# Seven block products in place of eight for the gate and up projections of a two-layer decoder trunk

## The chip, the cores and the metric

The kernel runs on one core of one Trainium2 chip. The metric is the time of one execution on the device in microseconds (us); several runs of the same kernel are taken and their median is quoted. A profile is one more execution, recorded instruction by instruction on each engine: TensorE (PE, with its weight loads as PEld), VectorE (DVE), ScalarE (ACT), GpSimd (POOL) and SyncE (SP), which here issues the loads from memory.

## What is computed

Two decoder layers over 512 tokens of width 1024. A layer has four sub-layers, each with an RMS norm in front and one behind: a feed-forward block, a token mixer (block-sparse attention beside retention), cross-attention into 256 memory tokens, and a second feed-forward block. The change is in the feed-forward blocks, of which there are four in all:

```python
D_MODEL = 1024; SEQ = 512; DEPTH = 2; D_FF = 2816

def swiglu(x, w_gate, w_up, w_down):
    return (jax.nn.silu(x @ w_gate) * (x @ w_up)) @ w_down

def rms_norm(x, g):
    xf = x.astype(jnp.float32)
    y = xf * lax.rsqrt(jnp.mean(xf * xf, axis=-1, keepdims=True) + EPS)
    return (y * g.astype(jnp.float32)).astype(x.dtype)

# in each layer, twice:
# x = x + 0.5 * rms_norm(swiglu(rms_norm(x, pre_g), w_gate, w_up, w_down), post_g)
```

All data are float32.

## The kernel before

Activations lie with features on the 128 partitions and the 512 tokens along the free axis: `x[c]`, eight tiles for 1024 features. Every large product is made of three matmuls in a reduced float32 type: each operand is split into a rounded part and the rest (`hi`, `lo`), and `mm3` adds hi·hi, hi·lo and lo·hi into one PSUM tile. The split of a weight tile of 128x1024 (`unit`: one load on SP's queue into `raw`, ACT writes `hi`, DVE writes `lo` = raw − hi) is done as the weights stream in; three `raw`, four `hi` and four `lo` buffers rotate. A normed input is not scaled before its product: `split_x` splits x times the gain of each feature, and the factor of each token (`bc`, from `prenorm`) is applied behind the product.

A feed-forward block (`ffn`) goes over the 22 blocks of 128 hidden features in three groups (8, 7, 7). For each block f the gate and the up product are 8 x 3 matmuls each, with 512 tokens moving past a stationary 128x128 weight tile. Then DVE and ACT form silu(gate)·up and split it into `hh`, `hl`. When a group is done, the down product adds its blocks into the eight output tiles y[c], again 512 tokens at a time; y is kept in SBUF and added to by DVE. In the last block of the kernel the first f and the last group are done in two halves of 256 tokens. Behind the last group: `sumsq`, `rms_cols`, and `postnorm`, which for each c forms yn (DVE), adds it to x (POOL, the first on DVE) and splits the new x for the next sub-layer. Products with the memory tokens (`mem_keys`, `mem_values`) are put in as fillers at the changes of sub-layer.

The program is written in order; a planner orders each engine's instructions before the run by its own costs, and places waits on semaphores where one engine needs another's result. On an engine the order is then fixed. SBUF is shared out in slots: tag `b` 24 tiles of 128x512, `xs` 16, `h` 16; PSUM as four tiles `acc` and four tiles `aux`.

The order of the two instructions that recur most:

```python
act.activation(hi, raw, AF.Copy)                                  # L85, whi
dve.tensor_tensor(lo, raw, hi.bitcast(F32), op=ALU.subtract)      # L86, wlo
```

Of the kernel before, what the change touches and what calls it, by code (L numbers as in the profile page):

```python
# [25 lines left out]
GROUPS = ((0, 8), (8, 15), (15, 22))  # L26
# [21 lines left out]
def trunk(ctx: ExitStack, tc: tile.TileContext, a: dict, out: bass.AP):  # L48
# [9 lines left out]
    slots = {"b": 24, "xs": 16, "h": 16, "kv": 6}  # L58
# [20 lines left out]
    def unit(src, n):  # L79

        raw = wp.tile([P, 1024], F32, name="raw", tag="raw", bufs=3)[:, :n]
        nc.sync.dma_start(raw, src)
        hi = wp.tile([P, 1024], F32R, name="whi", tag="whi", bufs=4)[:, :n]
# [5 lines left out]
    def raw_unit(src, n):  # L89
        raw = wp.tile([P, 1024], F32, name="raw", tag="raw", bufs=3)[:, :n]  # L90
        nc.sync.dma_start(raw, src)
        return raw
# [3 lines left out]
    nc.sync.dma_start(x[0], a["xT"][0])  # L96
    first = {0: unit(a["ffn1_gu"][0, 0, 0], 1024)}
    for c in range(1, 4):
        nc.sync.dma_start(x[c], a["xT"][c])
    first[1] = unit(a["ffn1_gu"][0, 0, 1], 1024)  # L100
    for c in range(4, NC):
        nc.sync.dma_start(x[c], a["xT"][c])
    nc.sync.dma_start(cst, a["consts"])
# [9 lines left out]
    def mm3(ps, ah, al, bh, bl, start, stop):  # L113
        pe.matmul(ps, ah, bh, start=start, stop=False)  # L114
        pe.matmul(ps, ah, bl, start=False, stop=False)  # L115
        pe.matmul(ps, al, bh, start=False, stop=stop)  # L116
# [40 lines left out]
    def rms_cols(ssq, n, width):  # L157
# [9 lines left out]
        return newton(v, nt)  # L167
# [17 lines left out]

    def gcols(l, col):
        return small[l][:, col : col + NC]

    def prenorm():

        xh, xl = [h for h, _ in xs], [lo for _, lo in xs]
        xs.clear()
        ssq, part = None, None
# [9 lines left out]
        return xh, xl, cols, bc  # L203

    def postnorm(y, ssq, gains, nxt, ts_=slice(0, T)):

        w = ts_.stop - ts_.start
        ps = row_bc(rms_cols(ssq[:, ts_], D, w), w // P)
        for c in range(NC):
# [3 lines left out]
            split_x(c, nxt, ts_)  # L213
# [43 lines left out]
    def ffn(l, which, gains, nxt, filler=None, prep=None, halves=False):  # L257
        gu, dn = FF_UNITS[which]
        if filler:
            filler()  # L260
        xh, xl, cols, bc = prenorm()
        y, ssq = [None] * NC, None
        for gi, (f0, f1) in enumerate(GROUPS):
            hh, hl = [], []
            for f in range(f0, f1):
                w = [first.pop(b) if b in first else unit(a[gu][l, f, b], 1024) for b in range(2)]
                pss = [acc("ps_gu") for _ in range(2)]
                for ts_ in HALVES if halves and f == 0 else (slice(0, T),):
                    for (wh, wl), ps in zip(w, pss):
                        for k in range(NC):  # L270
                            s = slice(k * P, (k + 1) * P)
                            mm3(ps[:, ts_], wh[:, s], wl[:, s], xh[k][:, ts_], xl[k][:, ts_], k == 0, k == NC - 1)
                g1 = big("g1")
                dve.tensor_tensor(g1, pss[0], bc, op=ALU.mult)  # L274
                th = big("th")
                act.activation(th, g1, AF.Tanh, scale=0.5)
                u1 = big("u1")
                dve.tensor_tensor(u1, pss[1], bc, op=ALU.mult)  # L278
                dve.scalar_tensor_tensor(g1, th, 1.0, g1, op0=ALU.add, op1=ALU.mult)
                dve.scalar_tensor_tensor(u1, g1, 0.5, u1, op0=ALU.mult, op1=ALU.mult)  # L280
                h_, l_ = split(u1, "h", tag="h")
                hh.append(h_)
                hl.append(l_)
            n = f1 - f0
            last = gi == len(GROUPS) - 1
            if prep and last:
                prep()
            if last and nxt is None:
                down_halves(a[dn][l], f0, n, hh, hl, y, gains)
                return  # L290
            for c in range(NC):
                wh, wl = unit(a[dn][l, c][:, f0 * P : f1 * P], n * P)
                ps = acc("ps_dn")
                for k in range(n):
                    s = slice(k * P, (k + 1) * P)
                    mm3(ps, wh[:, s], wl[:, s], hh[k], hl[k], k == 0, k == n - 1)
# [7 lines left out]
        postnorm(y, ssq, gains, nxt)  # L304

    def down_halves(src, f0, n, hh, hl, y, gains):

        w = []
        for c in range(NC):
            if c < 4:  # L310
                wh, wl = unit(src[c][:, f0 * P : (f0 + n) * P], n * P)
                w.append([(wh[:, k * P : (k + 1) * P], wl[:, k * P : (k + 1) * P]) for k in range(n)])
            else:
                raw = raw_unit(src[c][:, f0 * P : (f0 + n) * P], n * P)
                parts = []
                for k0 in (0, 4):
                    m = min(4, n - k0) * P
# [625 lines left out]
```

## Time and profile before

| what | value |
|---|---|
| median of three runs | 2507.27 us (2506.3 to 2509.06) |
| the profiled execution, its own time | 2508.29 us |
| its span, first to last instruction | 2506.5 us |
| mean granted clock of TensorE | 0.995 of full speed |
| PE, PEld, DVE, ACT, POOL busy | 97%, 81%, 56%, 36%, 10% of the span |

Times in the rows are in us from the start of the span, durations in us unless they are marked ns. "128x512 f32 x56 | 38.7, 691" means 56 instructions on tiles of 128 partitions by 512 elements, together 38.7 us, 691 ns each. Matmuls overlap, so the duration of one matmul is longer than the time from its start to that of the next; what a stretch of matmuls costs is the length of the stretch over their number.

### The profile page before, as it was taken

The numbers are of one execution on the slowest core, as the hardware profiler recorded it, in microseconds if no ns is written. First come the engines' busy times: TensorE is split into PE (matmuls) and PEld (weight loads), VectorE is DVE, ScalarE is ACT, GpSimd is POOL, SyncE is SP. The second block draws the span as 40 slices with busy tenths as digits, with TensorE's granted clock in tenths as the row PEclk, the third lists the DMA queues.
The fourth block names the chain that finished last, engine by engine and source line by source line (L and its number), as shares of the span: only waits on it lengthen the run. The fifth ranks groups of instructions, "written<-read, shape, count | busy, mean of one in ns | idle before, by whom it ended". The sixth has DMA issues, their size and how long they took to land. (4 is left out here: it accounts for less than half of the span.)

```text
span 2506.5 us, 30782 instructions
## 1 busy us (share of the span) xinstructions
PE 2431.5 (97%) x12052; PEld 2020.5 (81%) x12052; DVE 1400.2 (56%) x2536; ACT 902.4 (36%) x1480; POOL 258.8 (10%) x218
## 2 busy tenths in 40 slices
PE   8999999999999999999999999999999998999997
PEld 6888878888877878888878888868888777888887
DVE  6434458465776484344484344584657766634454
ACT  4322243255344443222343222332553443322222
POOL 0000022001040120000120000130010402100002
PEclk9999999999999999999999999999999999999999
DMA  4333333411232233233333333324112222232321
GB/s 173 98 100 94 99 121 108 143 45 34 76 109 84 93 101 93 101 93 100 110 98 96 101 93 101 106 89 150 44 35 70 93 76 68 86 100 92 102 90 62
DMA packets 74593, 233.62 MB, mean 93 GB/s; under 512 B 8272, under 2 KB 17744, under 8 KB 74448
## 3 DMA queue, kind: packets, MB, share of 16 engines
q1 hardware_dynamic: 65232, 222.21, 27.9%
q10 hardware_dynamic: 9216, 9.44, 1.2%
q8 instruction: 95, 1.56, 0.3%
q14 instruction: 50, 0.41, 0.1%
HBM read 229.53 MB, written 2.10 MB: 92 GB/s over the span
## 5 line engine op out<-in xcount | busy, mean ns | idle before, releaser
L85 ACT ACTIVATE whi<-raw 128x1024 fp32r<-128x1024 f32 (+2 forms) x402 | 417.8, 1041 | 1097.6 <-PE ps_gu L115 324.0
L86 DVE TENSOR_TENSOR wlo<-raw,whi 128x1024 fp32r<-128x1024 f32 (+2 forms) x402 | 491.2, 1223 | 292.7 <-ACT whi L85 284.4
L114 PE MATMUL ps_gu<-xsh,whi 128*128 128x512 f32 (+1 forms) x1424 | 552.3, 389 | 13.8 <-ACT whi L85 9.3
L115 PE MATMUL ps_gu<-xsl,whi 128*128 128x512 f32 (+1 forms) x1424 | 555.0, 390 | 9.9 <-DVE xsl L184 9.7
L116 PE MATMUL ps_gu<-xsh,wlo 128*128 128x512 f32 (+1 forms) x1424 | 552.8, 388 | 0.0
L115 PEld LDWEIGHTS ps_gu<-xsl,whi 128*128 128x128 f32 x1424 | 268.6, 189 | 71.2 <-DVE xsl L184 17.7
L114 PEld LDWEIGHTS ps_gu<-xsh,whi 128*128 128x128 f32 x1424 | 269.0, 189 | 69.2 <-ACT whi L85 9.2
L116 PEld LDWEIGHTS ps_gu<-xsh,wlo 128*128 128x128 f32 x1424 | 268.8, 189 | 55.4 <-DVE wlo L86 1.8
L154 POOL TENSOR_TENSOR ssq<-ssq,sq 128x512 f32<-128x512 f32 (+1 forms) x84 | 131.4, 1564 | 1708.7 <-ACT sq L153 1705.6
L115 PE MATMUL ps_dn<-hl,whi 128*128 128x512 f32 (+1 forms) x704 | 268.5, 382 | 2.4 <-DVE hl L123 2.4
L114 PE MATMUL ps_dn<-hh,whi 128*128 128x512 f32 (+1 forms) x704 | 268.2, 381 | 0.0
L116 PE MATMUL ps_dn<-hh,wlo 128*128 128x512 f32 (+1 forms) x704 | 268.0, 381 | 0.0
L278 DVE TENSOR_TENSOR u<-ps_gu,rstd_bc 128x512 f32<-128x512 f32 x88 | 60.8, 691 | 215.4 <-PE ps_gu L116 215.3
L274 DVE TENSOR_TENSOR g<-ps_gu,rstd_bc 128x512 f32<-128x512 f32 x88 | 60.8, 691 | 183.9 <-PE ps_gu L116 179.4
L115 PEld LDWEIGHTS ps_dn<-hl,whi 128*128 128x128 f32 x704 | 132.3, 188 | 28.9 <-DVE hl L123 3.8
L114 PEld LDWEIGHTS ps_dn<-hh,whi 128*128 128x128 f32 x704 | 132.4, 188 | 26.2 <-ACT hh L122 0.5
L116 PEld LDWEIGHTS ps_dn<-hh,wlo 128*128 128x128 f32 x704 | 132.4, 188 | 25.1
L301 DVE TENSOR_TENSOR y<-ps_dn,y 128x512 f32<-128x512 f32 x56 | 38.7, 691 | 132.3 <-PE ps_dn L116 132.3
L115 PE MATMUL ps_fm<-xsl,whi 128*128 128x512 f32 x256 | 103.2, 404 | 4.0 <-DVE xsl L184 3.8
L114 PE MATMUL ps_fm<-xsh,whi 128*128 128x512 f32 x256 | 103.0, 404 | 0.0
L116 PE MATMUL ps_fm<-xsh,wlo 128*128 128x512 f32 x256 | 101.3, 396 | 0.6 <-DVE wlo L86 0.6
L612 ACT ACTIVATE p<-p,smx 128x512 f32<-128x512 f32 (+3 forms) x128 | 70.5, 552 | 87.2 <-DVE smx L610 87.0
(226 smaller groups left out, 3723.0 us busy)
## 6 DMA issues: line engine op xcount, KB each, us to landing
raw<-in_ffn_gu_dram SPq DMA_DIRECT2D x176, 512.0 KB, 3.3
raw<-in_ffn_dn_dram SPq DMA_DIRECT2D x64, 448.0 KB, 3.3
raw<-in_ffn_dn_dram SPq DMA_DIRECT2D x32, 512.0 KB, 3.5
raw<-in_win_fm_dram SPq DMA_DIRECT2D x32, 512.0 KB, 3.3
raw<-in_wk_dram SPq DMA_DIRECT2D x16, 512.0 KB, 3.5
raw<-in_cmp_w_dram SPq DMA_DIRECT2D x16, 512.0 KB, 3.7
raw<-in_wout_dram SPq DMA_DIRECT2D x16, 512.0 KB, 3.5
raw<-in_wv_dram SPq DMA_DIRECT2D x16, 512.0 KB, 3.5
```

The lines of the kernel that those rows point to most:

```text
L85: act.activation(hi, raw, AF.Copy)
L86: dve.tensor_tensor(lo, raw, hi.bitcast(F32), op=ALU.subtract)
L114: pe.matmul(ps, ah, bh, start=start, stop=False)
L115: pe.matmul(ps, ah, bl, start=False, stop=False)
L116: pe.matmul(ps, al, bh, start=False, stop=stop)
L154: eng.tensor_tensor(acc_t, acc_t, sq, op=ALU.add)
L274: dve.tensor_tensor(g1, pss[0], bc, op=ALU.mult)
L278: dve.tensor_tensor(u1, pss[1], bc, op=ALU.mult)
L301: dve.tensor_tensor(y[c], ps, y[c], op=ALU.add)
L612: act.activation(pr[i], pr[i], AF.Exp, bias=m, scale=-1.0, accum_out=sums[:, i : i + 1])
```

## The change

The 2816 hidden features are taken in 11 pairs of blocks. For a pair, gate and up together are one product of a 2x2 block matrix of weights (two blocks of features by two halves of the 1024 inputs) with a 2x2 block matrix of inputs (two halves of the inputs by two halves of the 512 tokens). It takes eight block products by the usual rule and seven by Strassen's scheme (`p1` to `p7`). Each block product is 2 (gate, up) x 4 x 3 matmuls with 256 tokens moving. Sums of weight blocks are made by POOL in place in `raw`, before the split; sums of input blocks (`combos`) are made once for each feed-forward block; sums of products are made by DVE, ACT and POOL from PSUM. The up half is no longer scaled for each token; the factor is applied at the norm behind the block (`cols`). Gate and up of the first pairs are prepared ahead of the norm that precedes them (`ffn_first`). The down product follows after every two pairs (four blocks of h), so it has six groups, the last with one pair. Buffers: `b` 18, `xs` 24, `h` 8, `raw` 6.

```diff
-GROUPS = ((0, 8), (8, 15), (15, 22))
+NPAIR = NF // 2
+PAIRS = tuple(tuple(range(j, min(j + 2, NPAIR))) for j in range(0, NPAIR, 2))
-    slots = {"b": 24, "xs": 16, "h": 16, "kv": 6}
+    slots = {"b": 18, "xs": 24, "h": 8, "kv": 6, "onsa": 1}
...
+    def pair_tile(name):
+        t = wp.tile([P, 1024], F32, name=name, tag="raw", bufs=6)
+        return [t[:, :T], t[:, T:]]
...
-    def rms_cols(ssq, n, width):
+    def rms_cols(ssq, n, width, cols=None):
...
+        if cols is not None:
+            dve.tensor_tensor(t, t, cols[1], op=ALU.mult)
...
+    def direct(c, g, ts_=slice(0, T)):
+        k, top = c % 4, c < 4
+        if ts_.start == 0:
+            ops["x", c] = big("xg")
+        xg = ops["x", c]
+        act.activation(xg[:, ts_], x[c][:, ts_], AF.Copy, scale=g[:, c : c + 1])
+        if top:
+            if ts_.start == 0:
+                if k % 2 == 0:
+                    ops["t1", k // 2] = (big("x1h", F32R, tag="xs"), big("x1l", F32R, tag="xs"))
+                u = slice(k % 2 * 256, k % 2 * 256 + 256)
+                hi, lo = [t[:, u] for t in ops["t1", k // 2]]
+                act.activation(hi, xg[:, :256], AF.Copy)
+                dve.tensor_tensor(lo, xg[:, :256], hi.bitcast(F32), op=ALU.subtract)
+                ops[1, k] = hi, lo
+        else:
...
+            act.activation(hi, xg[:, ts_], AF.Copy)
+            dve.tensor_tensor(lo, xg[:, ts_], hi.bitcast(F32), op=ALU.subtract)
+            ops[3, k], ops[4, k] = [tuple(t[:, u] for t in ops["t3", k]) for u in HALVES]
+    def combos():
+        h7 = big("x7h", F32R, shape=(P, 4, T), tag="onsa")
+        for k in range(4):
...
+            pool.tensor_tensor(t7[:, :256], b[3], b[1], op=ALU.subtract)
+            dve.tensor_tensor(t5[:, :256], b[1], b[0], op=ALU.subtract)
+            dve.tensor_tensor(t5[:, 256:], b[3], t5[:, :256], op=ALU.subtract)
+            pool.tensor_tensor(t7[:, 256:], t5[:, 256:], b[2], op=ALU.subtract)
+            for o, t, hi in ((5, t5, None), (7, t7, h7[:, k])):
...
+                act.activation(hi, t, AF.Copy)
+                dve.tensor_tensor(lo, t, hi.bitcast(F32), op=ALU.subtract)
+                for u in range(2):
+                    ops[o + u, k] = hi[:, HALVES[u]], lo[:, HALVES[u]]
...
-        for c in range(NC):
+        for c in (0, 4, 1, 5, 2, 6, 3, 7) if nxt[0] else range(NC):
             t = big("yn")[:, :w]
             dve.scalar_tensor_tensor(t, y[c][:, ts_], gains[:, c : c + 1], ps, op0=ALU.mult, op1=ALU.mult)
             (dve if c == 0 else pool).tensor_tensor(x[c][:, ts_], x[c][:, ts_], t, op=ALU.add)
-            split_x(c, nxt, ts_)
+            follow(c, nxt, ts_)
...
+    class Pair:
...
+        def add(self, t, u):
+            pool.tensor_tensor(t, t, u, op=ALU.add)
+        def raw(self, n):
+            if n == 1:
+                self.a = self.load(0)
+            elif n == 2:
+                self.b = self.load(1)
+            elif n == 7:
+                self.c = self.load(2)
+                self.add(self.a, self.c)
+            elif n == 5:
+                self.d = self.load(3)
+                self.add(self.c, self.d)
+                return self.c
+            elif n == 6:
+                self.add(self.a, self.d)
+            elif n == 3:
+                self.add(self.a, self.b)
+            return self.b if n == 2 else self.d if n == 4 else self.a
...
+            for u in range(2):
+                for k in range(4):
+                    s = slice(u * 512 + k * P, u * 512 + (k + 1) * P)
+                    xh, xl = ops[o, k]
+                    mm3(ps[:, HALVES[u]], wh[:, s], wl[:, s], xh, xl, start and u == 0 and k == 0, u == 1 and k == 3, not start)
...
+        def p6(self):
+            self.product(6, self.B, 6, start=False)
+            self.e = big("ge")
+            dve.tensor_tensor(self.e, self.B, self.s1, op=ALU.subtract)
+            pool.tensor_tensor(self.s5, self.e, self.s5, op=ALU.subtract)
+        def p4(self):
+            self.product(4, self.C, 8, start=False)
+            dve.tensor_tensor(self.s7, self.e, self.s7, op=ALU.subtract)
+            dve.tensor_tensor(self.s5, self.s5, self.C, op=ALU.subtract)
+        def p3(self):
+            ps = acc("ps_gu")
+            self.product(3, ps, 4)
+            dve.tensor_tensor(self.e, ps, self.e, op=ALU.subtract)
+        def swiglu(self, bc, hs):
+            for q in ((self.A, self.e), (self.s5, self.s7)):
+                g1, th = big("g1"), big("th")
+                for ts_, t in zip(HALVES, q):
+                    dve.tensor_tensor(g1[:, ts_], t[:, :256], bc[:, ts_], op=ALU.mult)
+                act.activation(th, g1, AF.Tanh, scale=0.5)
+                dve.scalar_tensor_tensor(g1, th, 1.0, g1, op0=ALU.add, op1=ALU.mult)
+                for ts_, t in zip(HALVES, q):
+                    dve.tensor_tensor(g1[:, ts_], g1[:, ts_], t[:, 256:], op=ALU.mult)
+                hs.append(split(g1, "h", 0.5, tag="h"))
+    def ffn_first(l, which, filler=None):
+        def run():
+            if filler:
+                filler()
+            ps_ = warm[l, which] = [Pair(a[FF_UNITS[which][0]][l], j) for j in PAIRS[0]]
+            for n in (1, 2):
+                for p in ps_:
+                    p.weights(n)
+            ps_[0].r[7] = ps_[0].raw(7)
+        return run
...
+        for gi, js in enumerate(PAIRS):
+            if gi == 0:
+                ps_ = warm.pop((l, which))
+                for n in ("p1", "p2"):
+                    for p in ps_:
+                        getattr(p, n)()
+                for n in ("p7", "p5"):
+                    getattr(ps_[0], n)()
+                cols, bc = prenorm_rows()
...
+            for p in ps_:
+                for n in ("p1", "p7", "p5", "p2", "p6", "p4", "p3"):
+                    if gi > 0 or n not in ("p1", "p2") and (p is ps_[1] or n not in ("p7", "p5")):
+                        getattr(p, n)()
+                p.swiglu(bc, hs)
...
-        q = []
+        q = pair_tile("q") + pair_tile("q")
...
-            t = big("vr", tag="h")
+            t = big("vr", tag="xs")
```

## Rows read from the trace of the kernel before

**Rows 1.** The page, part 1: busy time of each engine, share, instructions.
```profile
PE 2431.5 (97%) x12052; PEld 2020.5 (81%) x12052; DVE 1400.2 (56%) x2536; ACT 902.4 (36%) x1480; POOL 258.8 (10%) x218
```

**Rows 2.** Busy time by stretch: length, PE, PEld, DVE, ACT, POOL, granted clock, DMA.
```profile
30.00:335.00 305.00, 305.00 (x1349) 252.52 (x1348) 142.22 (x172) 88.79 (x109) 0.00 (x0) 1.00 0.31 97
...
875.00:916.00 41.00, 36.88 (x204) 29.35 (x203) 36.37 (x61) 18.96 (x26) 16.85 (x10) 1.00 0.30 95
...
2110.00:2150.00 40.00, 31.71 (x188) 27.59 (x187) 33.00 (x83) 17.39 (x32) 15.69 (x17) 0.91 0.21 66
```

**Rows 3.** The same, PE, PEld, DVE on ps_gu (first) and ps_dn (others) alone.
```profile
145.00:221.20 76.20, 76.16 (x336) 62.88 (x336) 8.99 (x13) 1.00 0.30 92
...
221.30:259.30 38.00, 38.00 (x168) 31.22 (x167) 4.84 (x7) 0.00 (x0) 1.00 0.33 106
...
2476.60:2492.30 15.70, 15.70 (x131) 15.58 (x130) 2.44 (x6) 0.00 (x0) 1.00 0.20 68
```

**Rows 4.** Groups by line and shape: count | busy us, mean ns | idle before.
```profile
L86 DVE TENSOR_TENSOR wlo<-raw,whi 128x1024 fp32r<-128x1024 f32 x46 | 56.2, 1222 | 37.0 <-ACT whi L85 36.9
...
L301 DVE TENSOR_TENSOR y<-ps_dn,y 128x512 f32<-128x512 f32 x56 | 38.7, 691 | 132.3 <-PE ps_dn L116 132.3
...
L280 DVE SCALAR_TENSOR_TENSOR u<-g,u 128x512 f32<-128x512 f32 x88 | 61.2, 696 | 2.2
...
L123 DVE TENSOR_TENSOR hl<-u,hh 128x512 fp32r<-128x512 f32 x88 | 60.3, 685 | 9.8 <-ACT hh L122 9.8
...
L122 ACT ACTIVATE hh<-u 128x512 fp32r<-128x512 f32 x88 | 55.7, 633 | 63.2 <-DVE u L280 63.1
...
L329 DVE TENSOR_TENSOR y<-ps_dn,y 128x256 f32<-128x256 f32 x16 | 6.7, 422 | 18.9 <-PE ps_dn L116 18.7
...
L154 POOL TENSOR_TENSOR ssq<-ssq,sq 128x256 f32<-128x256 f32 x19 | 14.8, 777 | 654.4 <-ACT sq L153 654.1
```

**Rows 5.** Timeline of DVE within a group: start, duration, instruction, [idle before <- releaser].
```profile
2162.33 0.69 DVE L278 TENSOR_TENSOR u<-ps_gu,rstd_bc 128x512 f32<-128x512 f32 x1 [1.58 <-PE ps_gu L116]
2163.05 0.69 DVE L280 SCALAR_TENSOR_TENSOR u<-g,u 128x512 f32<-128x512 f32 x1
2163.66 1.22 DVE L86 TENSOR_TENSOR wlo<-raw,whi 128x1024 fp32r<-128x1024 f32 x1
2164.80 0.68 DVE L123 TENSOR_TENSOR hl<-u,hh 128x512 fp32r<-128x512 f32 x1
```

**Rows 6.** Timeline of POOL, and of DVE beside it, cross-attention to feed-forward.
```profile
354.74 1.29 POOL L154 TENSOR_TENSOR ssq<-ssq,sq 128x512 f32<-128x512 f32 x1 [2.18 <-ACT sq L153]
...
887.14 11.39 POOL L212 TENSOR_TENSOR x<-x,yn 128x512 f32<-128x512 f32 x7 [13.57 <-DVE yn L211]
898.49 5.66 POOL L154 TENSOR_TENSOR ssq<-ssq,sq 128x512 f32<-128x512 f32 x3
...
899.34 1.98 DVE L86 TENSOR_TENSOR wlo<-raw,whi 128x1024 fp32r<-128x1024 f32 x1
901.25 1.75 DVE L184 SCALAR_TENSOR_TENSOR xsl<-x,small,xsh 128x512 fp32r<-128x512 f32 x1
902.92 1.77 DVE L154 TENSOR_TENSOR ssq<-ssq,sq 128x512 f32<-128x512 f32 x1
904.62 0.74 DVE L184 SCALAR_TENSOR_TENSOR xsl<-x,small,xsh 128x512 fp32r<-128x512 f32 x1
905.28 0.68 DVE L154 TENSOR_TENSOR ssq<-ssq,sq 128x512 f32<-128x512 f32 x1
```

**Rows 7.** The same transition, ps_gu alone: length, PE, PEld, DVE, clock, DMA.
```profile
885.60:915.20 29.60, 22.15 (x85) 15.03 (x85) 0.00 (x0) 1.00 0.26 87
```

**Rows 8.** The end of the chain that ended last: start, duration, what.
```profile
2492.42 0.43 DVE y L329
...
2497.36 0.68 PE bc_ps L173 x2
...
2502.33 0.87 POOLq L938
```

More of the change, by code (lines that the diff above doesn't have):

```diff
@@ L111, in trunk, with mm3 @@
             lst.append(hg)
[L113 to L116, printed above, removed]
+    def mm3(ps, ah, al, bh, bl, start, stop, more=False):
+        pe.matmul(ps, ah, bh, start=start, stop=False, skip_group_check=more)
+        pe.matmul(ps, ah, bl, start=False, stop=False, skip_group_check=more)
+        pe.matmul(ps, al, bh, start=False, stop=stop, skip_group_check=more)
     def split(src, name, gain=None, tag="b"):
@@ L186, in gcols, with follow @@
+    def follow(c, nxt, ts_=slice(0, T)):
+        seven, g = nxt[:2]
+        (direct if seven else split_x)(c, g, ts_)
+        if seven and c == NC - 1 and ts_.stop == T:
+            combos()
     def gcols(l, col):
@@ L255, in out_halves, with __init__, load, weights @@
             postnorm(y, ssq, gains, nxt, ts_)
-    def ffn(l, which, gains, nxt, filler=None, prep=None, halves=False):
+    class Pair:
+        def __init__(self, src, j):
+            self.src, self.j, self.w, self.r = src, j, {}, {}
+        def load(self, q):
+            k = self.j, q
+            return first.pop(k) if k in first else raw_unit(self.src[self.j, q], 1024)
+        def add(self, t, u):
[17 more added lines that the diff above has]
+            return self.b if n == 2 else self.d if n == 4 else self.a
+        def weights(self, n):
+            self.w[n] = split_unit(self.r.pop(n) if n in self.r else self.raw(n))
+        def product(self, n, ps, o, start=True):
+            if n not in self.w:
+                self.weights(n)
+            wh, wl = self.w.pop(n)
+            for u in range(2):
[3 more added lines that the diff above has]
+                    mm3(ps[:, HALVES[u]], wh[:, s], wl[:, s], xh, xl, start and u == 0 and k == 0, u == 1 and k == 3, not start)
+        def kept(self, ps):
+            t = big("gk")
+            act.activation(t, ps, AF.Copy)
+            return t
+        def p1(self):
+            self.A = acc("ps_gu")
+            self.product(1, self.A, 1)
+            self.s1 = self.kept(self.A)
+        def p2(self):
+            self.product(2, self.A, 3, start=False)
+        def p7(self):
+            self.C = aux("ps_gc")
+            self.product(7, self.C, 7)
+            self.s7 = self.kept(self.C)
+        def p5(self):
+            self.B = acc("ps_gu")
+            self.product(5, self.B, 5)
+            self.s5 = self.kept(self.B)
+        def p6(self):
[21 more added lines that the diff above has]
+                hs.append(split(g1, "h", 0.5, tag="h"))
@@ L258, in ffn @@
+    warm = {}
+    def ffn_first(l, which, filler=None):
[8 more added lines that the diff above has]
+        return run
+    def ffn(l, which, gains, nxt, prep=None):
         gu, dn = FF_UNITS[which]
-        if filler:
-            filler()
-        xh, xl, cols, bc = prenorm()
@@ L262, in ffn @@
         y, ssq = [None] * NC, None
[L263 to L285, printed above, removed]
@@ new lines, in ffn @@
+        for gi, js in enumerate(PAIRS):
[7 more added lines that the diff above has]
+                cols, bc = prenorm_rows()
+                sq = tiny("cols2", NT)
+                dve.tensor_tensor(sq, cols, cols, op=ALU.mult)
+            else:
+                ps_ = [Pair(a[gu][l], j) for j in js]
+            hs = []
+            for p in ps_:
[3 more added lines that the diff above has]
+                p.swiglu(bc, hs)
+            f0, n = 2 * js[0], len(hs)
+            last = gi == len(PAIRS) - 1
@@ L818, in xattn @@
                     mm3(ps, v_h[:, fs], v_l[:, fs], pTh[m], pTl[m], m == 0, m == 1)
-                h_, l_ = split(ps, "xo", tag="h")
+                h_, l_ = split(ps, "xo", tag="xs" if f < 4 else "h")
                 oh.append(h_)
```

127 lines of the change are left out of this document (70 added, 57 removed).

## Prediction

> **What bounds the kernel now.** I read the page's busy shares first, then the stretches, then the groups, then the timeline where stretches meet. By the shares TensorE is busy for 97% of the span and no other engine for more than 56% [rows 1]. A matmul counts as busy longer than its place in the pipe, so I looked at a stretch: in 305 us inside a feed-forward block PE has no gap, DVE is busy 142 us, ACT 89 us and POOL not at all [rows 2]. So the inside of a block is bound by PE, and there the time follows the number of matmuls and the spacing of their starts. Where sub-layers meet it is another engine: in the 41 us from cross-attention to the second feed-forward block DVE is busy 36.4 us and POOL 16.9 us [rows 2], and 85 matmuls of gate and up took 29.6 us [rows 7] where inside a block they would take 19.3 us. A change that takes work from PE and gives it to DVE and POOL gains in the first kind of stretch and loses in the second.
>
> **The change part by part: matmuls.** 336 matmuls of 512 tokens take 76.20 us, 226.8 ns each; in the down product 168 take 38.00 us, 226.2 ns. 131 matmuls of 256 tokens, each with a weight load of its own, take 15.70 us, 119.8 ns [rows 3]. Halving the columns does not halve the cost: the two lines differ by 107 ns for 256 columns, and some 13 ns stay with every matmul. PEld is busy for 15.58 of those 15.70 us, so weight loads have no slack left, but they keep up. One pair before: 4 products x 8 x 3 = 96 matmuls x 226.8 = 21.77 us. After: 7 x 24 = 168 x 119.8 = 20.13 us. That is 7.5% less, not the eighth that the count of columns promises: 1.64 us. 43 pairs make 70.5 us. The 44th, first in the last block, has half of its 512-token matmuls split into halves today (48 x 226.8 + 96 x 119.8 = 22.39 us): 2.3 us. In that block the halved last group of down products shrinks from seven blocks to two: 360 x 226.2 + 336 x 119.8 ns = 121.7 us become 480 x 226.2 + 96 x 119.8 = 120.1 us: 1.6 us. Sum for PE: **74.4 us less**. Above 129.6 ns for a matmul of 256 tokens (96 x 226.8 / 168) nothing would be left of it.
>
> **Load on DVE and POOL in a pair.** Weight splits: 7 x 1.22 us where there were 4. Sums of products: three with an operand in PSUM (0.69 each) and one in SBUF (0.69). Gate: eight half-width steps of 0.42, two of 0.70, two splits of 0.69. Together 17.5 us of DVE; before it was 4 x 1.22 + 10 x 0.69 = 11.8 us [rows 4]. POOL: four sums of 128x1024, which the trace does not have; 256 columns take 0.78 us [rows 4] and 512 alone 1.29 [rows 6], so 1024 at the same slope 2.3 us, and one of 1.29: 10.5 us where there was nothing. The outputs y are added to by DVE five times in a block and not twice: 24 more at 0.69, 16.6 us a block. ACT gets some 3 splits and 3 copies more; it is at 36% and stays uncounted.
>
> POOL and DVE get in each other's way. Three additions on POOL, 1.29 us each alone, took 5.66 us; beside them a weight split took 1.98 (1.22 alone), an input split 1.75 (0.74), an addition 1.77 (0.68) [rows 4, 6]. Alone these would be 3.87 + 2.64 = 6.51 us; from 898.49 to 904.62 they took 6.13, a rate of 1.06, almost one after the other. I count POOL and the DVE instructions with two operands in SBUF as one queue. (The Trainium skill, SBUF — State Buffer, section "Who interferes with whom", has this as a lock: a DVE instruction with two SBUF inputs and a GpSimd instruction that reads SBUF exclude each other for a whole instruction. The trace agrees within those 6%; by the lock alone 6.13 would be 6.51, and the stretches below 6% longer.)
>
> A full group of two pairs: PE 2 x 20.13 + 96 x 0.226 = 62.0 us (65.3 before). The queue: DVE 2 x 14.5 + 4.9 for the down weights, POOL 21.0, together 54.9 us. It fits with 7 us to spare, so inside a block I keep PE as the bound.
>
> **Where a group turns to its down product.** The last product p3 has to become h before the third of four blocks can be multiplied: e 0.69, times bc 0.42, tanh 0.63 (as L122, the same shape), 0.70, two half steps 0.84, hi 0.63, lo 0.69: 4.6 us, with hand-overs of up to 0.1 as in [rows 5] 4.7 us. Now one step of the sort (u, product, split) hides behind seven earlier blocks. After it, PE has the first two blocks for three outputs, as many as PSUM has free: 18 x 0.226 = 4.1 us. It costs nothing if the planner finds more, 3.3 us if it keeps to one output at a time (6 matmuls, 1.4 us); I take 4.7 − 4.1 = 0.6, since the planner mixes accumulations already: 20 full groups, **12 us** (0 to 66). The last group of each block is one pair, and no h is ready: 4.7 us bare, four times, **18.8 us** (0 if memory products, put there as fillers, come early, to 24 with the other half of the pair's gate in the way).
>
> **The start of a block.** Count from the first yn, just before POOL's seven additions to x [rows 6]. Before, 29.6 us later 85 of the 192 matmuls of two pairs are done [rows 7]; the other 107 take 24.3 us, so the two pairs end at 53.9. After, four products (11.5 us) need only splits of x. The others need the sums of inputs, behind the last x at about 13 us: 8 half-width differences on each of DVE and POOL and 8 splits, to about 23 us. Then ten products, 28.8 us: 51.8 if nothing else is late, a cost of 1.2 us against the 3.3 gained in two pairs. But the queue has, up to there: POOL 7 x 1.29 + 8 x 0.78 + 3 x 1.29 + 7 x 2.3 + 2 x 1.29 = 37.8 us, DVE x 0.69, input splits 4 x 0.42 + 4 x 0.69, differences 3.4, their splits 5.5, squares 2.8, 15 weight splits 18.3, sums 1.4, gate of the first pair 5.3: 41.8 us. 79.6 us at the rate of 1.06 are 75 us. What is not due by then (gate 5.3, three down splits 3.7, a sum 1.3) or fits in the 13.57 us that POOL sat idle before [rows 6] (two weight splits 2.4) leaves 66.9, or 63 us: a cost of 12.4. Between 1.2 and 12.4 (24 if nothing can be put off) I take 6: the queue weighs here, but the first block has no additions to x, part of POOL's work lies under DVE instructions with an operand in PSUM (yn, e), and six of the sixteen late splits may slip behind products that wait anyway. Four blocks: **24 us** (5 to 56).
>
> **The rest.** At the end the last half has 48 matmuls (5.8 us) where it had 168 (20.1 us) over the norm of the first half. From the last matmul's sum (2492.42) to the last issue (2502.33) [rows 8] DVE carries everything; the first half's yn and additions now fall into it: **3 us** (0 to 8). Six more `xs` and fewer `b` slots: q and ksel move out of `b` by as many tiles in the mixer, so nothing there; in cross-attention nothing moves out, and a head could wait for one split (1.3 us, rows above, eight heads): 0, at most 10. Loads: the same bytes. A pause of PE can cost clock: with its bubble the start of the last block ran at a granted 0.91 [rows 2], which is 2.4 GHz with stretches of 1.2 GHz; 0, at most 4 us a block, within the bound of 56.
>
> Sum: −74.4 + 12 + 18.8 + 24 + 3 = −16.6 us on the profiled execution's 2508.29 us: 2491.7. That execution is 1.0 us above the median of the runs, so I give **2491 us**, 0.65% less.
>
> **Rivals.** *The queue of DVE and POOL sets the time* (slower). For it: rows 6, and the 36 of 41 us in which DVE is busy there already. Against: inside a block 7 us of each 62 are spare. A block's start costs 14 us, and as the products alone (40.3 us) face some 38 us of queue, each of the 16 later full groups slips by 1 us: −74.4 + 56 + 16 + 12 + 18.8 + 3 = +31, 2539 us (2512 to 2556). It decides from about 10 us a start. The skill's lock, above, would have this outcome if no work could be put off. *Everything is covered*: the planner fills the turns, and starts cost 1.2 us: −74.4 + 5 + 3 = −66, 2441 us. For it: no gap in 305 us today; against: a chain of 4.7 us with nothing ready in a one-pair group. *Gain and losses cancel*: a start costs 10 us: 2507. *It does not do what it says*, the matmuls coming no faster than 129.6 ns: 131 matmuls in a row speak against it; I give it no chance of its own.
>
> **How the numbers follow.** Forecast 0.40 (own range 2450 to 2501), all covered 0.12, cancelled 0.12, slower 0.36. What a measurement of this kernel can tell from no change is about 0.2%, 5 us. Faster 0.52, within 0.12, slower 0.36. The range leaves out the lower half or so of "all covered" and the upper quarter of the slow case: 2446 to 2546.
>
> **What would show it.** In the profile after: some 119.8 ns from start to start in ps_gu inside a block; PE still near 97%, or, if the queue wins, gaps before ps_gu released by DVE's whi/wlo or POOL's sums; POOL at 10 us a pair, weight splits near 1.22 us if they meet few of POOL's sums and near 2 us if many; a gap of 1 us at most before ps_dn in a full group and of 4 to 5 us in the last; two pairs done 55 to 60 us after the first yn. I am wrong if the starts cost over 10 us, or if the turns cost 3 us each.

## The result: ten per cent slower

| | before | after |
|---|---|---|
| median of the runs | 2506.84 us (2506.3 to 2509.06) | 2757.16 us (2754.84 to 2759.32) |
| ratio | | 1.0997, 95% interval [1.0977, 1.1016] |
| span of the profiled execution | 2506.5 us | 2755.6 us |
| mean granted clock of TensorE | 0.995 | 0.944 |

The prediction said 2491 us, 2446 to 2546. The time is 211 us above its upper end. The page of the changed kernel, part 1 (read as in [rows 1]):

```profile
PE 2460.6 (89%) x15052; PEld 2175.9 (79%) x15052; DVE 1943.3 (71%) x3090; ACT 1135.3 (41%) x1800; POOL 812.0 (29%) x470
```

PE has fallen from 97% to 89%; no other engine is near full. So no engine's total sets the time: PE stands in waits, and its clock falls. The clock has two levels here, 2.4 GHz and 1.2; by the means in the table some 309 us of the span were at the lower one, and 25 before. The table reads the stages from the starts and ends of their matmuls (a block from its first ps_gu to its last ps_dn, a mixer with cross-attention from its first ps_fm to its last ps_o), and gives the change of each.

| stage, us | before | after | change |
|---|---|---|---|
| four feed-forward blocks | 368.0, 368.4, 369.3, 376.4 | 415.2, 415.7, 415.3, 424.1 | +188.2 |
| two mixers with cross-attention | 476.6, 463.2 | 488.2, 477.4 | +25.8 |
| five turns between stages | 21.8, 12.7, 12.9, 12.3, 1.4 | 27.3, 20.3, 21.3, 14.4, 1.9 | +24.1 |
| after the last matmul of a down product | 14.1 | 24.9 | +10.8 |

Inside a block I looked at the first group, a full group, its down product, the last group of one pair, and its down product (windows of the second block; columns as in [rows 2]):

```profile
960.70:1037.30 76.60, 53.20 (x345) 50.02 (x346) 62.62 (x80) 36.58 (x55) 40.00 (x26) 0.78 0.19 62
...
1129.10:1175.70 46.60, 42.30 (x338) 41.89 (x337) 35.22 (x36) 19.76 (x25) 16.82 (x7) 0.96 0.35 107
1175.50:1197.70 22.20, 22.20 (x100) 17.87 (x99) 17.73 (x23) 6.79 (x9) 7.19 (x3) 1.00 0.21 65
...
1336.10:1356.40 20.30, 20.29 (x169) 20.09 (x167) 15.21 (x19) 11.23 (x17) 3.88 (x2) 1.00 0.57 173
1356.40:1376.40 20.00, 13.08 (x50) 10.03 (x51) 14.74 (x23) 9.64 (x16) 6.00 (x5) 0.83 0.35 110
```

The fourth line is the price that the prediction gave: 168 matmuls of 256 tokens without a gap in 20.3 us, 120 ns each. A full group's 336 should take 40.4 us and take 46.6; PE is idle for 4.3 of them, and the granted clock of 0.96 says that some of the rest ran at 1.2 GHz and not at 2.4. The first group takes 76.6 us at a clock of 0.78. In the last line PE stands for 6.9 us in all, at the turn to the down product. Per block that is 36.2 us in the first group, 4 x 6.3 in the full ones and 9 in the last, against some 18 us that PE saves and 8 that PE lost in the first group before.

What PE waits for in a full group, from the timeline of DVE, POOL, ACT and PE (start, duration, instruction, [idle before <- releaser]):

```profile
1144.64 1.41 DVE L407 TENSOR_TENSOR gk<-ge,gk 128x512 f32<-128x512 f32 x1
1146.62 2.78 DVE L90 TENSOR_TENSOR wlo<-raw,whi 128x1024 fp32r<-128x1024 f32 x1 [0.57 <-ACT whi L89]
1150.59 0.69 DVE L408 TENSOR_TENSOR gk<-gk,ps_gc 128x512 f32<-128x512 f32 x1 [1.19 <-POOL gk L403]
1151.19 2.80 DVE L90 TENSOR_TENSOR wlo<-raw,whi 128x1024 fp32r<-128x1024 f32 x1
1153.92 0.68 DVE L413 TENSOR_TENSOR ge<-ps_gu,ge 128x512 f32<-128x512 f32 x1
1154.63 0.42 DVE L420 TENSOR_TENSOR g<-ge,rstd_bc 128x256 f32<-128x256 f32 x1
...
1143.09 5.22 POOL L342 TENSOR_TENSOR raw<-raw 128x1024 f32<-128x1024 f32 x2 [6.17 <-DVE wlo L90]
1148.27 2.29 POOL L403 TENSOR_TENSOR gk<-ge,gk 128x512 f32<-128x512 f32 x1
1150.51 2.40 POOL L342 TENSOR_TENSOR raw<-raw 128x1024 f32<-128x1024 f32 x1
...
1155.09 0.63 ACT L421 ACTIVATE th<-g 128x512 f32<-128x512 f32 x1 [4.69 <-DVE g L420]
...
1158.89 0.58 ACT L378 ACTIVATE gk<-ps_gu 128x512 f32<-128x512 f32 x1
...
1159.52 0.39 PE L124 MATMUL ps_gu<-x3h,whi 128*128 128x256 f32 x1 [1.46 <-ACT gk L378]
```

Follow it downwards. A weight split is 1.22 us [rows 4]; beside POOL's sums the two here take 2.8. The second ends at 1153.99, and `e` of product p3 starts only there (1153.92), though PE had gone on to the next product at 1149.26. `g` follows, then ACT's tanh, which had ACT standing for 4.69 us with the queue behind it; in that queue is `gk`, the copy `kept` of p1, and only when p1 is copied may p2 add to the same bank of PSUM: PE stands for 1.46 us. The longer stand of this group comes a little later in the same way, between p5 and p6. A half step of the gate, 0.42 us [rows 4], meets POOL's next sum and takes 2.5 (two steps, 2.84 in all); ACT's `hh` waits for it, and the copy of p5 stands behind `hh`:

```profile
1160.51 2.84 DVE L424 TENSOR_TENSOR g<-g,gk 128x256 f32<-128x256 f32 x2
...
1159.35 3.38 POOL L342 TENSOR_TENSOR raw<-raw 128x1024 f32<-128x1024 f32 x1 [6.43 <-DVE wlo L90]
...
1163.38 0.63 ACT L135 ACTIVATE hh<-g 128x512 fp32r<-128x512 f32 x1 [2.48 <-DVE g L424]
...
1164.86 0.58 ACT L378 ACTIVATE gk<-ps_gu 128x512 f32<-128x512 f32 x1
...
1165.49 0.58 PE L124 MATMUL ps_gu<-x5h,whi 128*128 128x256 f32 x1 [2.84 <-ACT gk L378]
```

Of the whole kernel's waits two lines belong here (engine, line, waited for: us, times, longest). The first is ACT waiting for POOL's sum before it can split it, the second PE waiting for the copies:

```profile
ACT whi L89 <- POOL raw L342: 209.0, 84, 4.4
...
PE ps_gu L124 <- ACT gk L378: 70.6, 36, 2.9
```

Two thirds of the second line, 47.1 us, are the waits before p6, and 23.5 those before p2 (by the operands, x5h and x3h, on the page). And the groups of the page:

```profile
L90 DVE TENSOR_TENSOR wlo<-raw,whi 128x1024 fp32r<-128x1024 f32 x530 | 789.7, 1492 | 336.6 <-ACT whi L89 333.6
...
L342 POOL TENSOR_TENSOR raw<-raw 128x1024 f32<-128x1024 f32 x176 | 455.8, 2591 | 734.5 <-DVE wlo L90 696.2
```

A mean split is 1492 ns, 0.27 us above [rows 4]; POOL's sum is 2.59 us where the prediction had 2.3.

### The profile page after: what moved, and what is told of

The parts are those of the page before. It is cut to its first block, busy times and chain, and to the rows that moved or that the text cites. A ratio compares the mean times of both kernels' runs of the same rounds, so it can differ in the third digit from the quotient of the medians.

```text
span 2755.6 us, 38138 instructions
## 1 busy us (share of the span) xinstructions
PE 2460.6 (89%) x15052; PEld 2175.9 (79%) x15052; DVE 1943.3 (71%) x3090; ACT 1135.3 (41%) x1800; POOL 812.0 (29%) x470
## 5 line engine op out<-in xcount | busy, mean ns | idle before, releaser
L90 DVE TENSOR_TENSOR wlo<-raw,whi 128x1024 fp32r<-128x1024 f32 x530 | 789.7, 1492 | 336.6 <-ACT whi L89 333.6
L89 ACT ACTIVATE whi<-raw 128x1024 fp32r<-128x1024 f32 x530 | 556.9, 1055 | 806.7 <-POOL raw L342 209.0
L342 POOL TENSOR_TENSOR raw<-raw 128x1024 f32<-128x1024 f32 x176 | 455.8, 2591 | 734.5 <-DVE wlo L90 696.2
L124 PE MATMUL ps_dn<-hh,whi 128*128 128x512 f32 (+1 forms) x720 | 271.5, 396 | 27.6 <-ACT hh L135 22.6
L124 PE MATMUL ps_gu<-x5h,whi 128*128 128x256 f32 x704 | 214.2, 304 | 58.8 <-ACT gk L378 47.1
L124 PE MATMUL ps_gu<-x3h,whi 128*128 128x256 f32 x704 | 204.7, 291 | 23.5 <-ACT gk L378 23.5
L124 PE MATMUL ps_gc<-x7h,whi 128*128 128x256 f32 x704 | 206.0, 293 | 19.3 <-ACT whi L89 16.1
L125 PE MATMUL ps_gu<-x5l,whi 128*128 128x256 f32 x704 | 210.7, 299 | 1.5 <-DVE x5l L243 1.5
L126 PE MATMUL ps_gu<-x5h,wlo 128*128 128x256 f32 x704 | 210.3, 299 | 0.0
L126 PE MATMUL ps_gc<-x7h,wlo 128*128 128x256 f32 x704 | 203.7, 289 | 2.2 <-DVE wlo L90 2.2
L125 PE MATMUL ps_gc<-x5l,whi 128*128 128x256 f32 x704 | 204.0, 290 | 1.3 <-DVE x5l L243 1.3
L124 PEld LDWEIGHTS ps_gu<-x5h,whi 128*128 128x128 f32 x704 | 146.7, 208 | 64.0 <-ACT gk L378 51.9
L124 PEld LDWEIGHTS ps_dn<-hh,whi 128*128 128x128 f32 x720 | 134.9, 192 | 62.7 <-ACT hh L135 30.7
L124 PEld LDWEIGHTS ps_gu<-x3h,whi 128*128 128x128 f32 x704 | 138.5, 197 | 27.2 <-ACT gk L378 27.2
L124 PEld LDWEIGHTS ps_gc<-x7h,whi 128*128 128x128 f32 x704 | 141.3, 201 | 20.5 <-ACT whi L89 16.7
```

The costliest lines, as they stand in the source:

```text
L124: pe.matmul(ps, ah, bh, start=start, stop=False, skip_group_check=more)
L125: pe.matmul(ps, ah, bl, start=False, stop=False, skip_group_check=more)
L126: pe.matmul(ps, al, bh, start=False, stop=stop, skip_group_check=more)
L342: pool.tensor_tensor(t, t, u, op=ALU.add)
```

## The experiments

Theory: POOL's sums hold DVE up, and with it everything that stands in order behind DVE. The expectations of the first three runs call it Q, against O, the order of work at the start of a block; those of the fifth to seventh call it K, against C, the chain of sum, split, sum, split with its hand-overs from engine to engine. Beside it the layout, which the change brings along, has a price of its own. Each run is compared with the kernel before on the same chip.

**No sums of weights** (products 7, 5, 6 and 3 then use unsummed weights).

```
         def add(self, t, u):
-            pool.tensor_tensor(t, t, u, op=ALU.add)
+            return
```

> The changed kernel (2757 us), with the sums of weight blocks left out: POOL adds nothing in raw, the same weights are split in its place, so the products are not the right ones, and PE, ACT and DVE have the same instructions. Theory Q (the sums on POOL block DVE's weight splits and make them late): POOL loses 176 sums, 456 us; the gate and up stretch of a full group falls from 46.7 us to 41 or less, 16 groups give 90 to 100 us, the starts of the four blocks some 10 us each: 2610 to 2640. Rival O (the order of work at the start of a block: fillers ahead of the norm, the norm's sum of squares in the middle of the products): the groups behind the first keep 46 us and the time stays above 2720.

Measured: 2615.93 us (2614.28 to 2616.87), ratio 1.0428 [1.0412, 1.0443]. The sums cost 141 us. Every full group now takes 40.5 us, the bare price, and a split has a mean of 1231 ns. The first groups still take 63 to 76 us.

```profile
1016.50:1057.00 40.50, 40.50 (x338) 40.49 (x337) 28.73 (x35) 20.77 (x26) 2.95 (x2) 1.00 0.36 111
```

**Norm ahead of the fillers.**

```
-        if ts_.start == 0 and len(nxt) == 3:
-            nxt[2]()
         ps = row_bc(rms_cols(ssq[:, ts_], D, w, cols), w // P)
+        if ts_.start == 0 and len(nxt) == 3:
+            nxt[2]()
```

> The changed kernel with one thing moved: the products with the memory tokens and the first weights of a feed-forward block come behind the norm's transposes in program order, not ahead of them. Theory O: in two blocks the norm waited 17.6 us from the last output product to the first yn where the kernel before took 10.0; the two come back to about 10 and the time falls by 10 to 15 us, to 2742 to 2748; the third start has no filler and keeps its time. Rival Q alone: no change beyond 5 us, since the wait is made up by DVE and POOL later.

Measured: 2758.76 us, 1.0999 [1.0981, 1.1018]: no change, so O's 10 to 15 us did not come. The first yn does come earlier, 14.5 us after the last output product where it was 17.6, but not at the 10 expected, and the turn as a whole takes 20.4 us as before (20.3). The trace shows what took 4.3 us of the norm: DVE's small steps of the norm, with four numbers a partition, now met two of POOL's sums.

```profile
945.24 0.16 DVE L178 TENSOR_SCALAR rms_v<-rms_s 128x4 f32<-128x4 f32 x1
945.44 2.40 DVE L142 TENSOR_SCALAR rs_i<-rms_v 128x4 int32<-128x4 int32 x1
947.87 0.17 DVE L144 TENSOR_SCALAR rs_y<-rs_i 128x4 int32<-128x4 int32 x1
948.08 2.21 DVE L147 TENSOR_TENSOR rs_t<-rs_y 128x4 f32<-128x4 f32 x1
...
945.40 4.86 POOL L342 TENSOR_TENSOR raw<-raw 128x1024 f32<-128x1024 f32 x2 [7.63 <-DVE rms_v L178]
```

Steps of 0.17 us took 2.40 and 2.21, until POOL's instruction had ended. It is not a share of speed that DVE loses here; it stands. That is the lock of the Trainium skill (SBUF — State Buffer, "Who interferes with whom"), which it states for a DVE instruction with two SBUF inputs beside a GpSimd one that reads SBUF, and for whole instructions. The step of 2.21 us has two inputs, and its row agrees. The one of 2.40 has one input; whether it, too, falls under that rule, the trace does not show.

**Sum of squares behind fourteen products**, so that PE does not stand at the norm's transposes early in the first group (`prenorm_rows()` and both swiglus are moved behind the group's products).

> The changed kernel with the sum of squares of x and its transposes moved behind the 14 products of the first two pairs. Theory O: the hole of 12.9 us in PE between the products of the first two pairs goes, 4 times 8 to 13 us come back, less a wait before the first down product of 3 to 6 us: 2715 to 2740. Rival Q: the same work of DVE and POOL is only done later and the first gate comes as late: within 10 us of 2757.

Measured: 2769.54 us, 1.1045 [1.1028, 1.1062]: worse. The first group shrank to 62.7 us, and PE then stood for 16.7 us before the first down product, since both gates were late. The hole moved.

**The layout alone**: the kernel before, eight products, with the new buffers and groups.

```
-GROUPS = ((0, 8), (8, 15), (15, 22))
+GROUPS = ((0, 4), (4, 8), (8, 12), (12, 16), (16, 20), (20, 22))
...
-    slots = {"b": 24, "xs": 16, "h": 16, "kv": 6}
+    slots = {"b": 18, "xs": 24, "h": 8, "kv": 6}
...
-        raw = wp.tile([P, 1024], F32, name="raw", tag="raw", bufs=3)[:, :n]
+        raw = wp.tile([P, 1024], F32, name="raw", tag="raw", bufs=6)[:, :n]
...
-        q = []
+        q = pair_tile("q") + pair_tile("q")
...
-        ksel = []
+        ksel = pair_tile("ksel")
```

> The kernel before, with the changed kernel's buffers (b 18, xs 24, h 8, raw 6; q and ksel in raw, half of the outputs in xs) and its down product in groups of four blocks, but its own eight products and 512-token matmuls. Theory L (the buffers cost what the mixers lost, 15 to 21 us each): mixers at 337 us and 339 us, 2540 to 2550 us in all, the feed-forward blocks within 5 us each. Rival (the mixers lost it to their neighbours, as the norm before them and the work left over from the block): mixers at 316 and 324 us, within 8 us of 2507.

Measured: 2566.40 us, 1.0232 [1.0217, 1.0248]; a miss by 16 us, on the side of a dearer layout. Read by stage against before: mixers +11.7 and +14.4, three turns +5 each, the end +10.6, the blocks +6 together. In the mixer SP's queue stands: the loads wait for a raw slot that frees only when ps_hid has used its weights (DMA queue's waits, first 81 us of the mixer):

```profile
SPq L91 <- PE ps_hid L463: 35.9, 2, 34.1
```

Before, the same wait there came to 14.5 us, 7.5 at most.

**Sums of weights on DVE**, the same numbers computed.

```
-            pool.tensor_tensor(t, t, u, op=ALU.add)
+            dve.tensor_tensor(t, t, u, op=ALU.add)
```

> The changed kernel with the four sums of weight blocks of a pair made by DVE and not by POOL, the same results. Theory K (POOL's sums cost by blocking DVE): nothing blocks any more, but DVE gets 4 x 1.22 us a pair, some 22 us where the products take 20.2, so a full group's products take 43 to 45 us, between the 46.7 of the changed kernel and the 40.5 without sums: 2660 to 2720. Theory C (each sum is a step in a chain of sum, split, sum, split, whatever else waits): a step is half as long, 1.2 us for 2.4 to 2.8, groups of 41 us: 2620 to 2650.

Measured: 2635.30 us (2630.27 to 2636.79), 1.0502 [1.0486, 1.0517]: 122 of the 141 us come back with the same work in it. On DVE a sum takes 1.24 us where POOL needed 2.59, and a full group runs at the bare price with DVE far from full:

```profile
1024.10:1064.50 40.40, 40.40 (x338) 40.40 (x337) 32.61 (x39) 20.08 (x25) 4.09 (x2) 1.00 0.37 112
...
L342 DVE TENSOR_TENSOR raw<-raw 128x1024 f32<-128x1024 f32 x176 | 216.0, 1236 | 8.8 <-DMA raw<-in_ffn_gu_dram 7.1
```

The time lies in the range of theory C and below that of K, which had expected DVE's own load to show with 43 to 45 us a group. So this run alone spoke against the blocking. The next two took chain and blocking apart.

**Sums aside**: POOL adds the same weights (896 of 1024 columns, in two halves) to a tile that nobody reads, and the products use unsummed weights. POOL is as busy, and no split waits for it.

```
-            pool.tensor_tensor(t, t, u, op=ALU.add)
+            for s in (slice(0, 448), slice(512, 960)):
+                pool.tensor_tensor(aside, aside, u[:, s], op=ALU.add)
```

> The changed kernel with POOL's sums made aside: for each sum of 1024 columns two additions of 448 that read the second weight block but write a tile that nobody uses, so the weights are not summed and no split waits for POOL, while POOL is as busy. Theory K: DVE's splits are blocked as before, 46 us a full group, 2700 to 2760. Theory C: without the chain as if there were no sums, 40.5 us a group, 2616 to 2640.

Measured: 2809.61 us, 1.1200 [1.1179, 1.1220], slower than the change itself, though no split waits for POOL's result. The place is another: the gate and up part of a full group takes its 40.5 us, and the down product 30.6 instead of 22.2. POOL's sums, which no split orders now, bunch up beside the last gate; its half steps of 0.42 us take 1.3 there, and PE stands for 5.9 us and then runs in part at 1.2 GHz (granted clock 0.89).

```profile
1049.43 9.94 POOL L345 TENSOR_TENSOR aside<-aside,raw 128x448 f32<-128x448 f32 x6
...
1055.76 1.35 DVE L423 TENSOR_TENSOR g<-ge,rstd_bc 128x256 f32<-128x256 f32 x1
1057.04 2.61 DVE L423 TENSOR_TENSOR g<-gk,rstd_bc 128x256 f32<-128x256 f32 x2
...
1050.40:1081.00 30.60, 24.73 (x99) 19.41 (x99) 18.82 (x18) 10.57 (x16) 10.93 (x8) 0.89 0.22 69
1080.80:1121.30 40.50, 40.50 (x338) 40.50 (x337) 30.21 (x33) 20.77 (x26) 16.15 (x11) 1.00 0.38 108
```

**An eighth of the sums**: POOL adds only the first 128 columns. The chain of waits stays, each sum in it is short, and the blocking is cut with it.

```
-            pool.tensor_tensor(t, t, u, op=ALU.add)
+            pool.tensor_tensor(t[:, :P], t[:, :P], u[:, :P], op=ALU.add)
```

> The changed kernel with POOL's sums cut to 128 of 1024 columns: every wait and hand-over of the chain stays, seven eighths of each sum are left out. Theory K: almost nothing blocks, 40.5 to 42 us a full group, 2616 to 2645. Theory C with the hand-overs as its cost: 44 us or more, over 2680.

Measured: 2615.95 us, 1.0431 [1.0415, 1.0446], the time without sums (2615.93). The hand-overs cost nothing:

```profile
L90 DVE TENSOR_TENSOR wlo<-raw,whi 128x1024 fp32r<-128x1024 f32 x524 | 645.9, 1234 | 372.2 <-ACT whi L89 371.3
...
L342 POOL TENSOR_TENSOR raw<-raw 128x128 f32<-128x128 f32 x176 | 102.3, 581 | 940.2 <-DVE wlo L90 889.6 <-DMA raw<-in_ffn_gu_dram 22.8 <-issue 18.3
```

POOL's instruction of 2.59 us now takes 0.58, and splits are back at 1.23. Of the two tests both speak for K: blocking without the chain costs as much, though at another place, and the chain with short sums costs nothing. What they do not part is a long sum's two effects within the chain, that DVE stands beside it and that the next split waits for it. The rows of the full group, above, show both; C falls in the form that has the hand-overs as the cost.

**Neither sums of weights nor of inputs** (products 5 to 8 use the plain inputs x3 and x4).

The sums and splits in `combos` go, beside the edit of the first run:

```
-            t5, t7 = big("xt"), big("xt")
...
+            for o in (5, 7):
                 for u in range(2):
-                    ops[o + u, k] = hi[:, HALVES[u]], lo[:, HALVES[u]]
+                    ops[o + u, k] = ops[3 + u, k]
```

> The kernel without sums of weight blocks, and without the sums of input blocks too: products 5 to 8 take the split x of products 3 and 4. What remains at a block's start is the norm, x and its split. Theory: of the 16 us by which a start is longer than with eight products when no weights are summed, the input sums and their splits are 10 to 16: 4 times, 2616 falls to 2555 to 2580. Rival (the start's order, with the norm's sum of squares amid the products, costs them): 2600 or more.

Measured: 2577.34 us, 1.0273 [1.0256, 1.0290]: 38.6 us less than with them: the two middle blocks are 6 us shorter, the first and the last 10 and 14. A first group still takes 64.1 us in the second block, 24 above the bare price: PE stands for 14.4 us of it, and for its 49.7 busy us 40.4 would do at 2.4 GHz.

```profile
911.90:976.00 64.10, 49.70 (x345) 47.43 (x346) 44.71 (x72) 35.47 (x55) 15.59 (x12) 0.81 0.25 74
```

**q and ksel in tiles of their own** in the layout alone (24 of b, 3 of raw, as before the change).

```
-        q = pair_tile("q") + pair_tile("q")
+        q = [big("q") for _ in range(4)]
...
-        ksel = pair_tile("ksel")
+        ksel = [big("ksel") for _ in range(2)]
```

> Eight products in groups of four (2566.4), but q and ksel in b tiles of their own as before the change (24 of b, 3 of raw). Theory: q and ksel hold three of six raw slots in the mixer, and loads of win_fm wait for a slot; the mixers get their 24 to 26 us back, 2536 to 2546. Rival: the new places of vr, gr, o and xo in xs and h cost the mixers their time; 2560 to 2570.

Measured: 2545.32 us, 1.0157 [1.0142, 1.0173]: 21 us back, as the theory of raw slots had it. The mixers stand at 479.8 and 466.7 us.

**All sums on DVE**, those of inputs and of `s5` too, and the norm ahead of the fillers.

> As with the weight sums on DVE (2635.3), and the sums of inputs and s5 on DVE too, and the norm's transposes ahead of the fillers. Theory: POOL held DVE up at the starts as well; 2605 to 2625. Rival: at a start DVE has more work than fits whatever POOL does; 2628 to 2645.

Measured: 2616.40 us (2611.77 to 2619.56), 1.0438 [1.0420, 1.0455]: 19 us less than with the sums of weights alone on DVE, in the theory's range; which of the two edits gave it, the run cannot tell. The second block's first group takes 70.5 us still.

**Seven products only in groups two to five**: the first and last group by eight, sums on DVE, sums of inputs made while the first group runs. 32 of 44 pairs are then done by seven.

```
+            plain = gi in (0, len(PAIRS) - 1)
+            for p in ps_ if plain else ():
+                for f in range(2):
+                    w = [split_unit(p.load(2 * f + q)) for q in range(2)]
...
+                if gi == 0 and p is ps_[0]:
+                    combos(small[l][:, GPRE[which] : GPRE[which] + NC], xh, xl)
```

> Seven products only in groups two to five of a block, all their sums on DVE; the first and the last group by eight products, and the sums of inputs are made while the first group runs. Theory: the layout costs 58 us as measured and 32 pairs gain 1.64 us each, 52 us, with nothing lost at starts, in groups and at the turns: 2510 to 2525. Rival: DVE, with sums and splits in one queue, does not keep up in the middle groups either: 2535 to 2570.

Measured: 2530.16 us, 1.0096 [1.0081, 1.0111], 5 us above the theory's range: the blocks took 356.2 to 363.8 us, each 13 to 14 less than with eight products in this layout, where 8 x 1.64 is 13.1. The turn ahead of the second block, 20.3 us in the change, is back at 12.7. What the forecast missed lay in the mixers, 499.1 and 486.1 us; this version has one raw slot and two b slots fewer.

**The same with q in xs**, where the version above has four slots free in the mixer.

> The same with q in xs tiles, so that only ksel holds a raw slot. Theory of the raw slots: the mixers get most of 24 us back: 2486 to 2503, faster than before the change. Rival: places of vr, gr, o and xo: within 4 us of the run without this edit.

Measured: **2488.24 us** (2486.91 to 2491.26), 0.9931 [0.9916, 0.9946], faster than before. The mixers are at 476.6 and 466.3 us. A full group, and its share of DVE:

```profile
957.90:998.40 40.50, 40.50 (x338) 40.49 (x337) 33.10 (x42) 20.40 (x26) 0.00 (x0) 1.00 0.38 112
```

**The group of one pair fifth, not last.**

```
-PAIRS = tuple(tuple(range(j, min(j + 2, NPAIR))) for j in range(0, NPAIR, 2))
+PAIRS = ((0, 1), (2, 3), (4, 5), (6, 7), (8,), (9, 10))
...
-            plain = gi in (0, len(PAIRS) - 1)
+            plain = gi in (0, len(PAIRS) - 2)
```

> As the run with q in xs (2488.2), but the group of one pair is the fifth and a group of two pairs the last. Theory: the last down product of two blocks gives an output every 1.4 us, faster than squares and POOL's sums follow, and leaves 5.8 us to cover the first half's norm at the end; with four blocks the 5 us at each of three turns and 6 of the 10.5 us at the end come back: 2464 to 2472. Rival: groups of four as such, or the order of buffers, cost them: 2482 to 2492.

Measured: **2481.05 us** (2478.2 to 2482.64), 0.9891 [0.9874, 0.9907]; 7 us less and not 16 to 24, between the ranges. The three turns came back (22.9, 12.8 and 13.0 us, with 27.6, 16.7 and 16.8 before the edit), and so did 8 us at the end (16.8 from 24.9). But each block got 1 to 3 us longer: its last down product now follows a seven-product pair. In the second block it takes 25.8 us where others take 22.2, and PE stands for 2.9 of them, once for a weight split and once for the gate of the last pair. Splits of the memory tokens (`memg`) lie between on DVE; what they cost here was not tried.

```profile
1218.77 0.50 PE L124 MATMUL ps_dn<-hh,wlo 128*128 128x512 f32 x1 [1.13 <-DVE wlo L90]
...
1224.37 0.50 PE L122 MATMUL ps_dn<-hh,whi 128*128 128x512 f32 x1 [1.69 <-DVE g L397]
...
1217.00:1242.80 25.80, 22.86 (x100) 17.90 (x99) 20.14 (x29) 12.74 (x20) 9.86 (x6) 1.00 0.57 164
```

## Why the prediction was wrong

**PE's work: right.** 120 ns a matmul, no gap in the last group; with POOL's sums gone (no sums, sums on DVE) full groups cost the 40.4 us of it. The two versions with 32 pairs got 12 to 14 us a block back where 13.1 were due.

**"It fits with 7 us to spare, so inside a block I keep PE as the bound": the step that failed.** That the work fits is not what failed: DVE, its stands beside POOL counted in, is busy for 35.2 + 17.7 = 52.9 of the 68.8 us of a full group and its down product, and POOL for 24.0. (The prediction's 54.9 us cannot be held against these; they leave out DVE's work from PSUM.) But the step asked whether the work fits into the time, not what is late when DVE stands beside a sum of POOL that takes 2.6 us. A group has dates within it: p2 adds to the bank from which p1 must first be copied, and p6 to that of p5, and the copies stand in ACT's order behind a tanh and a split that wait for DVE. So 6.3 us and more were lost in each of 16 full groups, some 100 us, and the stretches at 1.2 GHz are part of that. The rival "queue of DVE and POOL sets the time" named the right engines, but by the same sum: 1 us a group. The runs show POOL's long sums as the cause, and blocking as its way: without the chain it costs as much, and with short sums the chain costs nothing.

**The start of a block: mechanism right, size not.** Predicted were two pairs done 55 to 60 us after the first yn; they end 79.3 us after it (957.97 to 1037.3). By the prediction's count, 53.9 less the 3.3 gained, that is a cost of 28.7 where "I take 6" stood, and above its bound of 24. The runs part it: in the second block a first group takes 76.6 us, 69.3 without sums of weights, 64.1 without those of inputs too, and 51.5 by eight products.

The clock, "0, at most 4 us a block", was a second term mis-sized. In this first group PE stands for 23.4 us, and it is busy for 53.2 where 40.4 would do: 12.8 us more, with the granted clock at 0.78. The group begins at the lower level, after a turn of 20.3 us; before the change the same start, after a turn of 12.7 us, ran at a clock of 1.00 [rows 2].

```profile
960.70:977.30 16.60, 9.54 (x35) 8.05 (x36) 12.19 (x17) 8.60 (x14) 10.99 (x10) 0.50 0.00 0
```

The 24 us above 40.4 that stay without any sum are made up likewise: 14.4 us in which PE stands and 9.3 that it is longer busy. Its waits there are for the split of x (`PE ps_gu L124 <- ACT x1h L217`, 9.5 us) and for the block's own norm (`PE bc_ps L188 <- DVE rs_y L151`, 4.7 us). That names places; what holds ACT and DVE up there was not tried and stays open.

**The turn to the down product: right in the middle, low in the last group.** In full groups PE goes on without a gap, with POOL's sums or without, and the down product takes 22.2 us where 96 matmuls by 0.226 are 21.7: as the prediction had it, the planner takes the first two blocks for several outputs, 21 matmuls ahead of the first that needs the third block. In the one-pair group I had 4.7 us bare; without sums PE stands 4.1 to 5.3 us, and beside POOL 4.1 to 6.9 us. The rest of that down product is slower too: in the second block 9 us are lost in it in all.

**The end: 3 us predicted, 10.8 measured.** After the last sum of y (2730.79) DVE and POOL still do the first half's yn and additions to x, then POOL the second half's squares (the chain that ended last, read as [rows 8]):

```profile
2735.39 0.84 POOL x L511
...
2737.35 0.68 POOL ssq L164
...
2742.06 0.44 DVE ssq L164
...
2751.50 0.88 POOLq L1115
```

The second half's squares come only after the first half's additions: from 2735.39 to 2742.06 the path is POOL's alone, 6.7 us. The layout alone, with eight products, ends 10.6 us later as well, so this is a price of the short last group. The last run gave 8 us of it back by a longer one, and with it the turns.

**Slots: 0 predicted, 26 us in the mixers.** "q and ksel move out of b by as many tiles in the mixer, so nothing there" looked at the pool they leave and not at the one they enter. They hold three of six raw slots, and loads of weights that stay there until ps_hid hold more; SP's queue stands in order behind one of them, in the layout run for up to 34 us. With the tiles back the mixers are within 3.5 us of before.

In sum, of the 249 us by which the span grew, about 141 are the sums of weights (122 of them only because POOL makes them), 58 the layout, and the rest starts and turns less what PE saves.

## What to carry to other kernels

Work given to an idle engine was not free here, since its instructions held up a busy one: count not only whether both fit into the stretch, but which instruction has a date and stands behind the longest single instruction of the other. When buffers change owner, ask who waits for a slot in the pool that they enter. A scheme that saves matmuls but needs sums of its inputs goes where the inputs have long been there, in the middle of a block, and not where a stage begins or ends.

## What was not expected of the hardware

A 128x4 step of DVE, 0.17 us alone, took 2.2 to 2.4 us where it met a 128x1024 sum of POOL. POOL's sum of 128x1024 takes 2.59 us in the mean and DVE's the same sum 1.24 us: moving it to the engine that seemed to be the fuller one cut the time by 4.4%.
